# A two-layer encoder trunk: all full feed-forward groups by seven products, with the 256-column remainder moved forward

## The chip, the cores and the metric

The kernel runs on one core of a Trainium2 chip. The metric is the device time of one execution in microseconds; the time before is the median of three runs. The profile is that of one further execution.

## The reference

Two layers over `x` of shape (1, 256, 1024), float32. Each layer is a half feed-forward, a mixing block with two kinds of attention, and another half feed-forward; so there are four feed-forwards, and a final RMSNorm. What the change touches is the feed-forward with 2816 hidden columns, and the closing norm:

```python
def rms_norm(x, g):
    xf = x.astype(jnp.float32)
    y = xf * lax.rsqrt(jnp.mean(xf * xf, axis=-1, keepdims=True) + RMS_EPS)
    return (y * g.astype(jnp.float32)).astype(x.dtype)

def swiglu(h, w_gate, w_up, w_down):
    return (jax.nn.silu(h @ w_gate) * (h @ w_up)) @ w_down

for l in range(DEPTH):
    x = x + 0.5 * swiglu(rms_norm(x, ffn1_norm[l]), ffn1_w_gate[l], ffn1_w_up[l], ffn1_w_down[l])
    ...   # h @ w_in, windowed attention with sinks, differential attention, @ w_out
    x = x + 0.5 * swiglu(rms_norm(x, ffn2_norm[l]), ffn2_w_gate[l], ffn2_w_up[l], ffn2_w_down[l])
return rms_norm(x, final_norm)
```

## The kernel before

**Numbers in two parts.** Every weight and activation is split into a high and a low part (`fp32r`), and a product of two tiles is three matmuls: high by high, low by high, high by low. ScalarE makes the high part of a weight (a cast), VectorE the low part (a subtraction); `emit_split` (L175) does half a weight tile of 128 x 4 x 512 at a time, so a weight step is two casts and two subtractions of 128 x 1024.

**The list of weight steps.** `specs` holds all weight tiles in order of use. `weights()` (L233) hands out the next one and calls `ahead` (L212), which issues splits up to `look[0]` half-steps further (8 in the feed-forwards, `IN_FFN`, falling to 6, `IN_MIX`, also the value elsewhere), and loads up to ten steps ahead as long as fewer than six raw tiles (`N_RAW`) are alive. `Split.part` (L166) calls `ahead` again when the second half of a step is first used, unless the step is held. The split tiles lie in a pool of 28 (`N_S4`).

**The order on the engines.** `Kept` (L40) keeps the instructions of TensorE, ScalarE, VectorE and GpSimd in program order in the feed-forwards, so each engine works through its queue as the program lists it, and an instruction that waits holds back all behind it.

**A feed-forward** (`ffn`, L566) works on five groups of 512 hidden columns and a remainder of 256. Group 0 and group 1 are plain: 96 matmuls of 512 columns (two token halves, eight row blocks, gate and up, three each). Then `gate` takes the SiLU on ScalarE and `up` multiplies on VectorE; at the next group `turn` (L634) transposes the hidden block on TensorE and splits it, and `down` (L648) adds its products with the down weights to four PSUM banks, 24 matmuls for each half of the output columns.

**Seven products.** Groups 2 to 4 (`SEVEN`) go by `by_seven` (L598): gate and up, the two halves of the rows and the two token halves form a 2 x 2 block product done with seven block products in place of eight, 12 matmuls each. That needs four sums of activation blocks (`make_sums`, L333; each a VectorE operation, a ScalarE copy and a VectorE subtraction), four sums of weight blocks (two made by accumulating loads from GpSimd's queue, `gather`, two by VectorE in place, `plus`, L130), seven split weight tiles in place of four, and VectorE's additions of the products (`put`). In the last of these groups some of the splits are postponed (`late`).

**The end.** After group 4 stands the remainder of 256 columns (48 matmuls); then `ffn_end` (L704) and `ffn_close` (L725) do the down products of group 4 and of the remainder (`tail`, 12 matmuls for each half of the columns), with the residual sum and the first transposes of the next norm between. The last feed-forward has an ending of its own: `close` adds the residual and takes squares on ScalarE, `finish` multiplies with the final gain and stores. The first feed-forward also takes in `x` (`take_x`, L410) and, in group 1, the constants for the attention (`attention_constants`, L475).

Of the kernel before, what the change touches and what calls it, by code (L numbers as in the profile page):

```python
# [9 lines left out]
F32 = mybir.dt.float32  # L10
# [20 lines left out]
SEVEN = (2, 3, 4)  # L31
# [3 lines left out]
def trunk(ctx: ExitStack, tc: tile.TileContext, x, n1, g1, u1, d1, nm, w_in, sink,  # L35
# [254 lines left out]
    class Norm:  # L290


        def __init__(self, g0, sums=len(SEVEN) > 0):
# [39 lines left out]
        def make_sums(self):  # L333
# [76 lines left out]
    def take_x(k):  # L410
# [8 lines left out]
        elif k == 1:  # L419
            for e in (g, u, g, u):  # L420
                next(e)
            norm.pair(2)
            ahead(5)
            norm.pair(3)
        elif k == 2:
            ahead(7)
            for t in range(2):
                for h in range(2):
                    norm.squares(t, h * 512, 512)
            norm.stats()  # L430
            constants()
# [134 lines left out]
    def ffn(norm, aside=None, before=None, final=False):  # L566
# [31 lines left out]
        def by_seven(h, g):  # L598
# [10 lines left out]
            act.copy(m7, prod(norm.summed(2), weights(held=True)))  # L609
            hT = turn(h, 2)  # L610
# [6 lines left out]
            p5 = prod(norm.summed(0), weights())  # L617
            late = g == max(SEVEN)
            p6 = prod(norm.summed(1), weights(look[0] - 5 if late else 0, late))
# [12 lines left out]
            return h  # L632
# [15 lines left out]
        def down(hT, g, h, w):  # L648
            tokens(accs[h], [None] * (2 * g) + hT, w, 4 * g, last=(FC - 1, G4 - 1) if final and h else FC - 1)

# [17 lines left out]
        for n in range(1, NGRP):  # L668
            sums = norm.make_sums() if n + 1 == min(SEVEN, default=0) else iter(())
            if n in SEVEN:  # L670
                look[0] = IN_FFN - max(0, n - 2)
                h = by_seven(h, n)
                continue
            gs = [bank(), bank()]
            tokens(gs, norm.xs, weights(), 0)
            hT = turn(h, 2)
            norm.copies()
            tokens(gs, norm.xs, weights(), 4)
            g = gate(gs)
            next(sums, None)  # L680
            us = [bank(), bank()]
            for k0 in (0, 4):
                tokens(us, norm.xs, weights(), k0)
                next(sums, None)
            h = hidden(g, us)
            for hh in range(2):
                down(hT, n - 1, hh, weights())
                if hh == 0:
                    next(sums, None)
                    if aside is not None:  # L690
                        aside()
                        aside = None
# [8 lines left out]
    BY_TOKENS = [(k, t) for t in range(2) for k in range(2)]  # L701
    G4 = 4 * (NGRP - 1)

    def ffn_end(parts, last):  # L704

        accs, hT, rest = parts
        hT = [None] * (2 * (NGRP - 1)) + hT
        hE = []
        look[0] = IN_MIX
        w = {0: weights()}  # L710

        def group(h, order, a=None, c=slice(None), first=0):
            tokens(a or accs[h], hT, w[h], G4, first=first, last=last[h], order=order, cols=c)

        def tail(h, order=BY_TOKENS, a=None, c=slice(None)):
            tokens(a or accs[h], [None] * (2 * NGRP) + hE, w["rest"], 4 * NGRP, last=last[h], order=order, cols=c, h=h)

        group(0, [(k, t) for k in range(3) for t in range(2)])
        hE.extend(rest())
        group(0, [(3, t) for t in range(2)])  # L720
        w["rest"] = weights()
        w[1] = weights(2)
        return group, tail

    def ffn_close(parts, nxt):  # L725
        group, tail = ffn_end(parts, (FC - 1, G4 + 3))
        res = Residual(nxt, parts[0])
        group(1, [(0, t) for t in range(2)])
# [9 lines left out]
        group(1, [(2, t) for t in range(2)])  # L738
        group(1, [(3, t) for t in range(2)])
# [231 lines left out]
    fss = const.tile([P, 2, 4], F32, name="fss")  # L971
    gf = []

    def final_gain():
        gf.append(blk(F32))
        sp.dma_start(gf[0].rearrange("p a n -> p (a n)"), nf.partition_broadcast(P))
        pool.memset(fss, 0.0)


    for l in range(DEPTH):  # L980
        final = l == DEPTH - 1
        parts = ffn(norm, attention_constants, take_x) if l == 0 else ffn(norm)
        norm_m = Norm(16 + l * 8, False)
        ffn_close(parts, norm_m)
        norm2 = Norm(32 + l * 8)
        mix(l, norm_m, norm2)
        parts = ffn(norm2, final_gain if final else None, final=final)
# [3 lines left out]


    def close(t, c0, n, acc):
# [4 lines left out]
        act.activation(jk[:, :n], xv, AF.Square, accum_out=fss[:, t, c0 // 256:c0 // 256 + 1])  # L998
# [3 lines left out]
    def finish(t):  # L1002
        rf = tmp("rf", 2, (P, 1))
        dve.tensor_reduce(rf, fss[:, t], axis=mybir.AxisListType.X, op=ALU.add)
        dve.tensor_scalar(rf, rf, 1.0 / D, EPS, op0=ALU.mult, op1=ALU.add)
        pool.tensor_tensor(rf, rf, mhalf[:, 0:1], op=ALU.pow)
# [3 lines left out]
        for j in range(2):  # L1010
            sp.dma_start(out[0, t * P:(t + 1) * P, j * 512:(j + 1) * 512], ob[:, j])
# [5 lines left out]
    tail(0)  # L1017
    for t in range(2):
        close(t, 0, 512, accs[0][t])
    group(1, [(k, 0) for k in (2, 3)])  # L1020
    tail(1, [(k, 0) for k in range(2)])
    close(0, 512, 512, accs[1][0])
    finish(0)
    for c in (0, 256):
        acc = bank()[:, 0:256]
        cols = slice(c, c + 256)
        group(1, [(k, 1) for k in range(4)], [None, acc], cols, G4)
        tail(1, [(k, 1) for k in range(2)], [None, acc], cols)
# [32 lines left out]
```

## Time and profile before

| | |
|---|---|
| median of three runs | 940.94 us (940.77 to 941.16) |
| the profiled execution | 938.1 us, span 936.3 us |
| TensorE busy | 922.1 us, 4796 matmuls, granted clock 0.997 |
| VectorE busy | 757.3 us |
| ScalarE busy | 573.2 us |
| HBM read | 192.71 MB |

The span is from the first to the last instruction; the execution's own time is 1.8 us longer. Busy times of engines overlap. In answers by stretch, each row gives a stretch of the span, then for each engine its busy time and number of instructions, then TensorE's granted clock, the DMA share and GB/s. In answers in order of time, a row gives start, length, engine, line, operation, output and inputs, number of instructions, and in brackets the engine's idle time before it and what ended it. All engine instructions bear the line of the helper `Kept` (L50), so they are told apart by their tiles: `w` split weights, `raw` weights as loaded, `s` activations and hidden blocks, `q` and `v` sums of activations, `tmp` intermediate results, `ps` PSUM banks, `xk` the residual stream.

### The profile page before, as it was taken

The page shows a single profiled execution, that of the slowest core. Times are in us where ns is not written, and L with a number is a line of the kernel's source. Part 1 is how long each engine was busy: PE and PEld are TensorE (multiplying, and loading weights), DVE is VectorE, ACT ScalarE, POOL GpSimd, SP SyncE. Part 2 cuts the span into 40 slices and gives each one's busy share as a digit, 9 for nine tenths or more (in the row PEclk, how much of TensorE's full clock was granted, in tenths as well). Part 3 has the DMA queues.
Part 4 walks back from the last instruction along what each step waited for, and adds up shares of the span by engine and source line. Part 5 has one row for each costly group of instructions (what it writes and reads, how often), then busy time and mean ns, then how long its engine had stood idle before and what let it go on. Part 6 is the DMA issues. An engine that isn't in the chain of part 4 may idle for free.

```text
span 936.3 us, 12676 instructions
## 1 busy us (share of the span) xinstructions
PE 922.1 (98%) x4796; PEld 782.2 (84%) x4796; DVE 757.3 (81%) x1066; ACT 573.2 (61%) x901; POOL 51.3 (5%) x73
## 2 busy tenths in 40 slices
PE   8999999999999999999999999999999999999997
PEld 6788778899898888888888888888999888888886
DVE  6679999859866588999866799996697566799992
ACT  6847675548745666576475565665577476466562
POOL 0400100000000000100001000000000001001001
PEclk9999999999999999999999999999999999999999
DMA  9986897928425857797667597887462467697821
GB/s 336 355 219 159 247 289 249 270 91 225 136 91 180 249 156 225 206 288 256 240 227 221 135 288 202 240 284 217 150 193 91 135 205 202 166 299 204 249 91 46
DMA packets 110893, 194.58 MB, mean 208 GB/s; under 512 B 3566, under 2 KB 31280, under 8 KB 110832
## 3 DMA queue, kind: packets, MB, share of 16 engines
q1 hardware_dynamic: 96816, 167.27, 53.3%
q0 software_dynamic: 12928, 25.46, 15.4%
q10 hardware_dynamic: 1088, 1.05, 0.3%
q8 instruction: 37, 0.61, 0.3%
q14 instruction: 24, 0.20, 0.1%
HBM read 192.71 MB, written 1.05 MB: 207 GB/s over the span
## 4 chain that ended last, share of the span: by engine, by line
PE 92%; DMA 4%; DVE 1%; ACT 1%; issue 1%; SPq 0%; ACTq 0%; POOLq 0%; POOL 0%; DVEq 0%
PE ps L50 92%; DMA raw<-in_ffn_w_up_dram 2%; DMA raw<-in_ffn_w_gate_dram 2%; DVE w L50 1%; DMA xk<-in_x_dram 1%; ACT w L50 0%; DVE tmp L50 0%; ACT junk L50 0%; DVE s L50 0%; ACT tmp L50 0%; SPq L152 0%; ACT L50 0%; ACTq L50 0%; DVE xk L50 0%; POOLq L1056 0%
## 5 line engine op out<-in xcount | busy, mean ns | idle before, releaser
L50 PE MATMUL ps<-w,s 128*128 128x512 f32 (+1 forms) x2754 | 642.1, 391 | 2.1 <-ACT tmp L50 2.1
L50 PEld LDWEIGHTS ps<-w,s 128*128 128x128 f32 x2754 | 512.7, 189 | 107.8 <-ACT tmp L50 2.6
L50 DVE TENSOR_TENSOR w<-raw,w 128x1024 fp32r<-128x1024 f32 (+1 forms) x440 | 460.8, 1093 | 57.0 <-ACT w L50 55.8
L50 ACT CAST w<-raw 128x1024 fp32r<-128x1024 f32 (+1 forms) x440 | 391.1, 948 | 85.8 <-DVE raw L50 71.0
L50 PE MATMUL ps<-w,q 128*128 128x512 f32 x432 | 101.9, 389 | 0.0
L50 PEld LDWEIGHTS ps<-w,q 128*128 128x128 f32 x432 | 81.1, 188 | 16.8
L50 PE MATMUL ps<-s,w 128*128 128x256 f32 x672 | 84.1, 285 | 0.0
L50 PEld LDWEIGHTS ps<-s,w 128*128 128x128 f32 x672 | 81.7, 192 | 1.1
L50 ACT ACTIVATE s<-ps,gcol 128x256 fp32r<-128x256 f32 (+1 forms) x80 | 31.5, 488 | 48.0 <-PE ps L50 48.0
L50 ACT CAST s<-ps 128x512 fp32r<-128x512 f32 x48 | 26.1, 593 | 51.9 <-PE ps L50 51.9
L50 DVE TENSOR_TENSOR raw<-raw,raw 128x1024 f32<-128x1024 f32 x48 | 56.4, 1216 | 0.0
L50 DVE TENSOR_TENSOR s<-ps,s 128x512 fp32r<-128x512 f32 x48 | 31.0, 684 | 27.1 <-ACT s L50 27.1
L50 POOL DMA_DIRECT2D raw<-in_ffn_w_up_dram x24 | 31.0, 1293 | 354.9 <-DVE w L50 163.2
L50 PE MATMUL ps<-ident,s 128*128 128x128 f32 x304 | 40.2, 274 | 1.4 <-DVE s L50 1.3
L50 PEld LDWEIGHTS ps<-ident,s 128*128 128x128 f32 x304 | 35.0, 141 | 7.2 <-DVE s L50 2.8
L50 ACT ACTIVATE tmp<-tmp,r 128x512 f32<-128x512 f32 x24 | 17.3, 722 | 35.5 <-DVE tmp L50 35.5
L50 ACT ACTIVATE s<-s,negm 128x256 f32<-128x256 f32 x64 | 31.9, 500 | 5.4 <-DVE negm L50 5.2
L50 PE MATMUL ps<-w,v 128*128 128x512 f32 x144 | 34.6, 389 | 0.0
L50 ACT CAST q<-tmp 128x512 fp32r<-128x512 f32 x20 | 12.4, 620 | 35.0 <-DVE tmp L50 34.9
L50 PEld LDWEIGHTS ps<-w,v 128*128 128x128 f32 x144 | 27.0, 188 | 5.6
L50 DVE SCALAR_TENSOR_TENSOR s<-ps,gcol,s 128x256 fp32r<-128x256 f32 x48 | 20.3, 478 | 12.3 <-ACT s L50 12.3
L50 DVE TENSOR_TENSOR xk<-xk,ps 128x512 f32<-128x512 f32 (+1 forms) x25 | 14.2, 598 | 17.6 <-PE ps L50 17.6
(107 smaller groups left out, 426.1 us busy)
## 6 DMA issues: line engine op xcount, KB each, us to landing
raw<-in_ffn_w_down_dram SPq DMA_DIRECT2D x44, 1024.0 KB, 6.0
raw<-in_ffn_w_gate_dram SPq DMA_DIRECT2D x39, 1024.0 KB, 5.9
raw<-in_ffn_w_up_dram SPq DMA_DIRECT2D x39, 1024.0 KB, 5.6
raw<-in_ffn_w_up_dram POOLq DMA_DIRECT2D x24, 1024.0 KB, 11.2
raw<-in_w_in_dram SPq DMA_DIRECT2D x14, 1024.0 KB, 5.5
raw<-in_ffn_w_gate_dram SPq DMA_DIRECT2D x8, 512.0 KB, 6.4
raw<-in_ffn_w_up_dram SPq DMA_DIRECT2D x8, 512.0 KB, 7.4
raw<-in_w_in_dram SPq DMA_DIRECT2D x8, 512.0 KB, 6.8
```

Of the source, the lines that this page charges most:

```text
L50: ins = issue(*a, **k)
```

## The change

All four groups 1 to 4 go by seven products in every feed-forward. The order becomes: group 0, the remainder of 256 columns, groups 1 to 4; its hidden block is kept (`hE`) and its down products come at the end, ahead of and between those of group 4. The four sums of activations are made during the remainder's stage, two in its middle and two behind it, in another order. In the first feed-forward three of the four squares are taken earlier, the look-ahead is 6 from group 2 on, and the attention's constants are made in `ffn_close`. In the last one the squares are summed on VectorE in one instruction that also multiplies, the factor of the mean is put into the gain by GpSimd, and the stores go out on two queues.

```diff
-            for g in range(1, NGRP):
-                downs = [down(g - 1, h) for h in range(2)]
-                if g in SEVEN:
-                    specs.extend(seven(wg[l], wu[l], g * 512, downs))
-                else:
-                    specs.extend(plain(w[l], g * 512, 512, k0, 4) for w in (wg, wu) for k0 in (0, 4))
-                    specs.extend(downs)
             for k0 in (0, 4):
...
                 specs.append(Step(4, 512, gu_moves))
-            specs.append(down(NGRP - 1, 0))
+            for g in range(1, NGRP):
+                specs.extend(seven(wg[l], wu[l], g * 512, [down(g - 1, h) for h in range(2)]))
             specs.append(plain(wd[l], 0, D, 4 * NGRP, 2))
-            specs.append(down(NGRP - 1, 1))
+            specs.extend(down(NGRP - 1, h) for h in range(2))
...
+            make(t1, t0, ALU.subtract)
+            yield
             s1 = make(b1, t1, ALU.subtract)
             yield
             s2 = make(s1, t0, ALU.add)
             yield
-            make(t1, t0, ALU.subtract)
-            yield
             make(b0, s2, ALU.subtract)
...
+            norm.squares(0, 0, 512)
             norm.pair(2)
+            norm.squares(1, 0, 512)
             ahead(5)
             norm.pair(3)
+            norm.squares(0, 512, 512)
         elif k == 2:
             ahead(7)
-            for t in range(2):
-                for h in range(2):
-                    norm.squares(t, h * 512, 512)
+            norm.squares(1, 512, 512)
...
-            hT = turn(h, 2)
+            hs = turn(h, 1 if g == 1 else 2)
+            if g > 1:
+                hT = hs
...
+        norm.copies()
+
+        sums = norm.make_sums()
         gu = [bank(), bank()]
         tokens(gu, norm.xs, weights(), 0)
         hT = turn(h, 2)
+        for _ in range(2):
+            next(sums)
         tokens(gu, norm.xs, weights(), 4)
         h = hidden(gate([b[:, 0:256] for b in gu]), [b[:, 256:512] for b in gu])
-        return accs, hT, lambda: turn(h, 1)
+        for _ in sums:
+            pass
+        hE, h = by_seven(hT, h, 1)
+        for n in range(2, NGRP):
+            look[0] = IN_FFN - (n - 2) if before is not take_x else IN_MIX
+            h = by_seven(None, h, n)[1]
+        look[0] = IN_MIX
+        return accs, hE, lambda: turn(h, 2)
...
+    def ffn_close(parts, nxt, aside=None):
+        accs, hE, turn_ = parts
+        res = Residual(nxt, accs)
+        we = weights(1)
+        tail(accs[0], hE, we, 0)
+        hT = turn_()
+        if aside is not None:
+            aside()
+        group(accs[0], hT, weights(1), ALL)
         for t in range(2):
             res.add(0, t)
-        tail(1)
-        ahead(2 * at["use"] - 2 + look[0])
-        group(1, [(1, t) for t in range(2)])
+        tail(accs[1], hE, we, 1)
+        w = weights()
+        group(accs[1], hT, w, ALL[:2])
         for j in range(2):
             nxt.pair(j)
         res.squares(0)
-        group(1, [(2, t) for t in range(2)])
-        group(1, [(3, t) for t in range(2)])
+        group(accs[1], hT, w, ALL[2:])
...
-        act.activation(jk[:, :n], xv, AF.Square, accum_out=fss[:, t, c0 // 256:c0 // 256 + 1])
+        s_ = tmp("tot", 4, (P, 1))
+        dve.tensor_tensor_reduce(out=jk[:, :n], in0=xv, in1=xv, scale=1.0, scalar=tot[t], op0=ALU.mult, op1=ALU.add,
+                                 accum_out=s_)
...
-        dve.tensor_reduce(rf, fss[:, t], axis=mybir.AxisListType.X, op=ALU.add)
-        dve.tensor_scalar(rf, rf, 1.0 / D, EPS, op0=ALU.mult, op1=ALU.add)
-        pool.tensor_tensor(rf, rf, mhalf[:, 0:1], op=ALU.pow)
+        pool.tensor_tensor(rf, tot[t], mhalf[:, 0:1], op=ALU.pow)
...
-        for j in range(2):
-            sp.dma_start(out[0, t * P:(t + 1) * P, j * 512:(j + 1) * 512], ob[:, j])
-
-    accs = parts[0]
-    group, tail = ffn_end(parts, ((FC - 1), FC - 1))
+        for j, q in enumerate((act, sp)):
+            q.dma_start(out[0, t * P:(t + 1) * P, j * 512:(j + 1) * 512], ob[:, j])
+
+    accs, hE, turn_ = parts
+    we = weights(1)
+    tail(accs[0], hE, we, 0)
+    tail(accs[1], hE, we, 1, (-1, FC - 1))
     dve.tensor_tensor(xk[:, 1, 512:D], xk[:, 1, 512:D], accs[1][1], op=ALU.add)
-    group(1, [(k, 0) for k in range(2)])
-    tail(0)
+    hT = turn_()
+    group(accs[0], hT, weights(), ALL)
...
```

More of the change, by code (lines that the diff above doesn't have):

```diff
@@ L564, in late, with ffn @@
                 self.nxt.stats()
-    def ffn(norm, aside=None, before=None, final=False):
+    def ffn(norm, before=None):
         def silu(out_, acc, t):
@@ L648, in down @@
         def down(hT, g, h, w):
-            tokens(accs[h], [None] * (2 * g) + hT, w, 4 * g, last=(FC - 1, G4 - 1) if final and h else FC - 1)
+            tokens(accs[h], [None] * (2 * g) + hT, w, 4 * g, last=-1)
         gs, us = [bank(), bank()], [bank(), bank()]
@@ L667, in ffn @@
         h = hidden(g, us)
[L668 to L692, printed above, removed]
+        norm.copies()
+        sums = norm.make_sums()
         gu = [bank(), bank()]
@@ L701, in trunk @@
+        return accs, hE, lambda: turn(h, 2)
     BY_TOKENS = [(k, t) for t in range(2) for k in range(2)]
+    ALL = [(k, t) for k in range(4) for t in range(2)]
     G4 = 4 * (NGRP - 1)
[L704 to L728, printed above, removed]
-        tail(0)
+    def tail(accs, hE, w, h, last=-1):
+        tokens(accs, [None] * (2 * NGRP) + hE, w, 4 * NGRP, last=last, order=BY_TOKENS, h=h)
+    def group(accs, hT, w, order, c=slice(None), first=0):
+        tokens(accs, [None] * (2 * (NGRP - 1)) + hT, w, G4, first=first, last=G4 + 3, order=order, cols=c)
+    def ffn_close(parts, nxt, aside=None):
[7 more added lines that the diff above has]
+        group(accs[0], hT, weights(1), ALL)
@@ L990, in trunk @@
             ffn_close(parts, norm)
+    tot = [tmp("tot", 4, (P, 1)) for _ in range(2)]
+    for t in range(2):
+        dve.memset(tot[t], D * EPS)
     def close(t, c0, n, acc):
@@ L1025, in trunk @@
         acc = bank()[:, 0:256]
[L1026 to L1028 removed]
+        group([None, acc], hT, w, [(k, 1) for k in range(4)], slice(c, c + 256), G4)
         close(1, 512 + c, 256, acc)
```

32 lines of the change are left out of this document (16 added, 16 removed).

## The prediction

> **What bounds the kernel now.** I read the page first, then the chain, then the busy time by stage, then the order in time around the places where one engine waits for another.
>
> ```profile
> span 936.3 us, 12676 instructions
> ...
> PE 922.1 (98%) x4796; PEld 782.2 (84%) x4796; DVE 757.3 (81%) x1066; ACT 573.2 (61%) x901; POOL 51.3 (5%) x73
> ...
> PE 92%; DMA 4%; DVE 1%; ACT 1%; issue 1%; SPq 0%; ACTq 0%; POOLq 0%; POOL 0%; DVEq 0%
> ```
>
> TensorE carries 92% of the chain, so a matmul removed should be time removed. VectorE's 81% looks like room. It is a mean over unlike stages, so the next view is busy time by stage: two seven-product groups of the first feed-forward, then of the second feed-forward group 0 and the seven-product groups 2, 3 and 4.
>
> ```profile
> core 0: us, PE busy (x) PEld busy (x) DVE busy (x) ACT busy (x) POOL busy (x), PEclk, DMA share, GB/s
> ...
> 99.60:131.90 32.30, 31.32 (x142) 25.58 (x141) 31.73 (x34) 20.02 (x23) 2.55 (x2) 1.00 0.87 245
> 131.90:163.40 31.50, 31.04 (x141) 25.35 (x140) 31.40 (x35) 19.16 (x23) 0.00 (x0) 1.00 0.84 255
> ```
>
> ```profile
> 293.60:315.50 21.90, 21.90 (x104) 18.20 (x103) 15.04 (x22) 16.96 (x28) 0.70 (x1) 1.00 0.72 232
> ...
> 350.60:381.40 30.80, 30.80 (x141) 25.60 (x140) 26.61 (x27) 17.99 (x21) 2.57 (x2) 1.00 0.84 232
> 381.40:412.30 30.90, 30.90 (x142) 25.64 (x141) 30.39 (x32) 19.46 (x23) 2.57 (x2) 1.00 0.82 241
> 412.30:443.10 30.80, 30.80 (x142) 25.59 (x141) 30.66 (x34) 20.26 (x24) 0.00 (x0) 1.00 0.82 247
> ```
>
> In the second feed-forward TensorE never stops, but VectorE is busy 26.61 of 30.80 us in group 2 and then 30.39 of 30.90 and 30.66 of 30.80. From the second seven-product group on VectorE is full. The change puts a fourth such group in that row. So the question is how much VectorE is behind, and the rows for that are the end of `up` (VectorE's last two products of a group, `s<-tmp,hr,tmp`) against the transposes (`ident`) of the next group that read them.
>
> ```profile
> 383.88 1.41 DVE L50 SCALAR_TENSOR_TENSOR s<-tmp,hr,tmp 128x512 f32<-128x512 f32 x2
> ...
> 415.53 1.42 DVE L50 SCALAR_TENSOR_TENSOR s<-tmp,hr,tmp 128x512 f32<-128x512 f32 x2
> ```
>
> ```profile
> 356.86 2.98 PE L50 MATMUL ps<-w,s 128*128 128x512 f32 x12
> ...
> 373.27 11.04 PE L50 MATMUL ps<-w,s 128*128 128x512 f32 x48
> 384.15 2.89 PE L50 MATMUL ps<-w,q 128*128 128x512 f32 x12
> 386.88 1.03 PE L50 MATMUL ps<-ident,s 128*128 128x128 f32 x8
> ...
> 417.71 1.03 PE L50 MATMUL ps<-ident,s 128*128 128x128 f32 x8
> ```
>
> Group 2's `up` ends at 385.29 and is read at 386.88: 1.59 us to spare. Group 3's ends at 416.95 and is read at 417.71: 0.76 us. TensorE's period is 417.71 - 386.88 = 30.83 us, VectorE's 416.95 - 385.29 = 31.66 us, and in that group the look-ahead had just been cut from 8 to 7, which saved VectorE one split. These are the last margins of the old kernel.
>
> **Part by part: TensorE.** Group 1 becomes seven products: 84 matmuls in place of 96. The pitch is (384.15 - 373.27) / 48 = 0.227 us, so 12 x 0.227 = 2.72 us for each of four feed-forwards, 10.9 us in all. The order of the stages and the places of the down products move matmuls without adding any.
>
> **VectorE.** What a group holds there:
>
> ```profile
> L50 DVE TENSOR_TENSOR w<-raw,w 128x1024 fp32r<-128x1024 f32 x18 | 21.3, 1217 | 0.4 <-ACT w L50 0.3
> L50 DVE TENSOR_TENSOR raw<-raw,raw 128x1024 f32<-128x1024 f32 x4 | 4.7, 1216 | 0.0
> L50 DVE TENSOR_TENSOR tmp<-ps,tmp 128x512 f32<-128x512 f32 x3 | 2.0, 682 | 0.0
> L50 DVE TENSOR_TENSOR tmp<-tmp,ps 128x512 f32<-128x512 f32 x3 | 2.0, 680 | 0.0
> ```
>
> A converted group splits 7 weight tiles, not 4 (6 more half-tile splits x 1.217 = 7.3 us), makes two sums of weights in place (4 x 1.216 = 4.9) and combines the products (7 x 0.68 = 4.8): 17.0 us more per feed-forward, against 2.72 us less of TensorE. None of it hides by itself where VectorE is full; it hides only if VectorE is ahead when the row of four begins. The next rows price a split in a full queue and the end of group 4.
>
> ```profile
> 443.20 1.41 DVE L50 SCALAR_TENSOR_TENSOR s<-tmp,hr,tmp 128x512 f32<-128x512 f32 x2
> 444.53 6.90 DVE L50 TENSOR_TENSOR w<-raw,w 128x1024 fp32r<-128x1024 f32 x6
> ...
> 448.52 1.03 PE L50 MATMUL ps<-ident,s 128*128 128x128 f32 x8
> ...
> 451.35 1.28 DVE L50 TENSOR_TENSOR s<-ps,s 128x512 fp32r<-128x512 f32 x2
> ```
>
> A split takes 6.90 / 6 = 1.15 us. VectorE's periods are therefore: with the look-ahead constant, 31.66 + 1.15 = 32.8 us; with one step less, 31.66; and for the last group, with its postponed splits, 444.61 - 416.95 = 27.66.
>
> **Entry into group 1.** Up to 325.06 us (the first group's `turn`) the old trace holds for the new order too, since TensorE has the same 24 matmuls ahead of it.
>
> ```profile
> 322.52 1.04 PE L50 MATMUL ps<-ident,s 128*128 128x128 f32 x8
> ```
>
> ```profile
> 323.77 1.29 DVE L50 TENSOR_TENSOR s<-ps,s 128x512 fp32r<-128x512 f32 x2 [3.10 <-ACT s L50]
> ...
> 330.40 0.69 DVE L50 TENSOR_TENSOR tmp<-s,s 128x512 f32<-128x512 f32 x1
> 331.77 0.69 DVE L50 TENSOR_TENSOR q<-tmp,q 128x512 fp32r<-128x512 f32 x1 [0.69 <-ACT q L50]
> ```
>
> ```profile
> 357.37 1.29 DVE L50 TENSOR_TENSOR s<-ps,s 128x512 fp32r<-128x512 f32 x2 [0.99 <-ACT s L50]
> ```
>
> One sum of tokens costs VectorE 332.46 - 330.40 = 2.06 us, 0.69 of it waiting for ScalarE's copy. Before, the four lay between splits over 35 us of group 1. After, they stand in pairs inside 11 us of the 256-column stage: two sums (4.1), two splits (2.3), two short `up` (about 1, half the shape of the long ones' 0.7 each), two sums (4.1), three splits (3.4), the `turn` of the narrow hidden block (0.7), and about 0.4 of waiting for casts: 325.0 + 16 = 341.0. TensorE ends that stage at 322.5 + 0.8 + 24 x 0.227 = 328.8, and starts the third product after two products and four transposes at 334.6. So VectorE is 341.0 - 334.6 = 6.4 us behind where in group 2 of the old kernel it was 358.66 - 356.86 = 1.8. It is 4.6 us later, and the spare was 1.6: the first transposes wait 3.0 us.
>
> **The row of four**, feed-forwards 2 and 3. Group 1 to 2: 3.0 us (above). Group 2 to 3, look-ahead 8 both times: 32.8 - 30.8 = 2.0. Group 3 to 4, cut to 7: 31.66 - 30.83 = 0.8. After group 4 the transposes come 12 matmuls later than the downs' end, not 24 as before, so TensorE arrives after 30.83 - 2.72 = 28.1 us and `up` after 27.66: no wait, 0.45 to spare. But the transposed block is now used at once, by `group(accs[0], ...)`; before, 24 matmuls stood between. Four splits stand ahead of it in VectorE's queue: 4 x 1.15 + 0.6 = 5.2 us after `up`, of which the 0.45 and the transposes' 0.9 are covered: 3.8 us. Sum 9.6 - 2.72 = +6.9 us each, +13.8 for both.
>
> **Feed-forward 4.** Both tails stand ahead of the transposes, so the last wait is 3.8 - 2.72 = 1.1: 3.0 + 2.0 + 0.8 + 1.1 - 2.72 = +4.2. The closing is shorter:
>
> ```profile
> 928.87 4.54 SPq L1011 DMA_DIRECT2D out_dram<-s  x4
> ...
> 929.79 0.42 DVE L50 TENSOR_TENSOR xk<-ps,xk 128x256 f32<-128x256 f32 x1 [0.58 <-PE ps L50]
> ...
> 931.27 0.56 POOL L50 TENSOR_TENSOR rf<-rf,mhalf 128x1 f32<-128x1 f32 x1 [3.18 <-DVE rf L50]
> ```
>
> Between the last add (ends 930.21) and the power (931.27) lie 1.06 us of ScalarE's square, its read-out and two small VectorE steps; one multiply-and-sum on VectorE, about as long as that add, with its read-out leaves some 0.6. With the last store on a queue of its own (one issue less, about 0.4) I take -0.9. Sum +3.3.
>
> **Feed-forward 1.** It has waits of its own now: the excess of the two stages over 30.83, 1.5 + 0.7 = 2.2, and this at the end of group 0:
>
> ```profile
> 31.00:33.20 2.20, 0.16 (x1) 0.16 (x2) 1.85 (x2) 2.18 (x3) 2.20 (x6) 1.00 1.05 387
> 33.20:36.70 3.50, 3.50 (x9) 2.72 (x10) 2.17 (x2) 3.50 (x5) 3.05 (x16) 0.51 1.06 376
> ```
>
> TensorE does 0.16 us of work in 2.20 (the gate's SiLU stands behind four squares), and then the granted clock is 0.51 for 3.5 us. With three squares moved ahead the wait goes (2.1 us) and, I take it, the slow clock with it (1.7). The new waits: 3.0; group 2 has two splits less (look-ahead 6), 30.5, so none and 0.3 gained; group 3 32.8, 1.7; group 4 27.66 + 1.15 - 28.1 = 0.7; the block at the end 5.2 - 0.9 = 4.3. Sum 9.7 - 2.72 - 2.1 - 1.7 - 2.2 = +1.0. The attention constants move behind the last transposes; they hide beside 48 matmuls, and cost up to 3 us if they do not.
>
> **Queues.** Eight more accumulating loads of 1 MB go through POOL. The DMA share in seven-product stages is 0.82 to 0.87 where the start shows 1.05, so I take zero; a late one costs at most what feed-forward 1 shows, 1 to 2 us. The final gain now waits on POOL before the last feed-forward, with its loads already issued: zero, or 1 us. A third product in group 1 may wait for the bank that ScalarE's copy frees: 0 to 1 us each, mostly inside the 3.0.
>
> **The sum**: +1.0 + 6.9 + 6.9 + 3.3 = +18.1 us. The profiled execution took 938.1 us, 1.8 outside its span, and would take 956.2. The median shown, 940.94, is 2.8 above that; 940.9 + 18.1 gives 959 us.
>
> **Rivals.** *Caught up at the entry*: if the sums hide and group 1 starts as group 2 did, each feed-forward loses 3.0 and the 1.6 of spare comes off the next wait: 4.6 x 4 = 18.4, and the time is 941, no change. For it speaks only that the old sums were hidden; against it that they wait on ScalarE in pairs now. *All hidden, faster*: the look-ahead of four to five weight steps swallows the fourth group. It decides where VectorE's surplus over four groups stays under its margin at the entry; then the waits stay out: -10.9 - 2.1 - 1.7 - 0.9 = -15.6, 925 us. For it: TensorE stood still nowhere in feed-forward 2. Against: 1.59 and then 0.76 us to spare after only two groups, and the uncovered block at the end, which no look-ahead helps. *Clock drops*: waits of 3.8 us may bring the half clock of the rows above behind each of the first three feed-forwards, 1.7 us each: 964 us. The Trainium skill ("TensorE: Matmul & The Clock Gate", Part 1) has the clock halved after an idle window of about 3.4 us; here an idle of 2.1 us was enough, so the measured row decides, and by either the wait is long enough.
>
> **How the numbers follow.** VectorE-bound as summed 0.68, clock drops on top 0.13, caught up 0.06, all hidden 0.13. The likeliest gives 959. Upward, bank waits (up to 4), constants (3) and the clock (5) are not all paid at once: 969. Downward, I take three quarters of the entry's 18.4 as hidden: 945; that leaves no change and 925 outside, less than 2 in 10 together. A difference under 0.2% (1.9 us) is no change. Faster 0.14, same 0.05, slower 0.81.
>
> **What would show it.** TensorE idle before the transposes of groups 2 and 3 with VectorE as releaser, and before the first matmuls of the last group's downs; VectorE above 30.3 of every 30.8 us in all four groups; the second and third feed-forwards some 7 us longer than before; no 2.1 us gap at 31 us. It is wrong if TensorE's idle stays near 14 us in all, or if VectorE has idle time at the start of group 1.

## The result and the profile after

The changed kernel takes 989.78 us (median of 4 executions, 988.47 to 990.68) against 940.86 us of the kernel before on the same chip: ratio 1.0519, 95% interval 1.05 to 1.0537. It is slower, as forecast, but by 49 us where 18 were forecast, and outside the range of 945 to 969. The profiled execution has a span of 988.9 us, 52.6 more than the one before.

The page of the changed kernel, with the rows that answer to those of before (the last is the chain by engine and line):

```profile
span 988.9 us, 12741 instructions
...
PE 934.1 (94%) x4742; PEld 781.1 (79%) x4742; DVE 822.9 (83%) x1142; ACT 594.7 (60%) x921; POOL 63.5 (6%) x81
...
PE 48%; DVE 21%; DMA 18%; issue 10%; ACT 3%; POOLq 0%; ACTq 0%; DVEq 0%; POOL 0%
PE ps L49 48%; DMA raw<-in_ffn_w_up_dram 18%; DVE w L49 12%; DVE tmp L49 5%; ACT w L49 2%; DVE s L49 2%; DVE raw L49 2%; DMA xk<-in_x_dram 0%; ACT s L49 0%; ACT q L49 0%; DVE q L49 0%; DVE xk L49 0%; ACTq L49 0%; DVEq L49 0%; ACT junk L49 0%
```

The records hold 54 matmuls fewer (48 of them the fourth group's four times 12), yet TensorE is busy for longer; one reason is that some of them ran at half clock. Its share of the chain falls from 92% to 48%. VectorE has 21%, which fits the forecast's mechanism, but the loads of the up weights have 18%, which the forecast had costed at nothing. The list of waits says the same; each row gives the total, the number of waits and the longest. First before, then after:

```profile
ACT w L50 <- DMA raw<-in_ffn_w_up_dram: 10.0, 9, 2.8
...
PE ps L50 <- DVE s L50: 1.3, 3, 0.7
```

```profile
ACT w L49 <- DMA raw<-in_ffn_w_up_dram: 49.0, 22, 10.1
...
PE ps L49 <- DVE s L49: 27.2, 24, 7.5
PE ps L49 <- DVE tmp L49: 11.2, 10, 2.4
```

To see where the time lies I cut each profiled execution at the first transposes of the residual (`ident,xk`) ahead of feed-forwards 2, 3 and 4. Before, these start at 299.85, 478.04 and 757.54 us. The mixing blocks in the first and third stretch hardly change, so the differences are those of the feed-forwards (the fourth with the closing):

| difference to before, us | FF1 | FF2 | FF3 | FF4 and closing | sum |
|---|---|---|---|---|---|
| forecast | +1.0 | +6.9 | +6.9 | +3.3 | +18.1 |
| after | +19.9 | +13.7 | +10.8 | +8.2 | +52.6 |
| a1, accumulating loads left out | +3.2 | +7.5 | +8.6 | +5.4 | +24.7 |
| d3, a seventh raw tile, nothing left out | +15.8 | +7.6 | +8.6 | +5.1 | +37.1 |
| a3, VectorE's weight sums left out | +7.8 | -1.2 | -1.4 | -0.5 | +4.7 |
| c3, new order, group 1 plain | +1.8 | +3.8 | +5.7 | +2.8 | +14.1 |
| f1, all remedies | +7.7 | +2.8 | +2.6 | +5.1 | +18.2 |
| f2, new order, group 1 plain, end mended | -2.8 | +0.4 | +0.3 | +2.1 | +0.1 |

(The profiled execution of before was 2.8 us under its median; on that account every measured sum is 2.8 us too high.) More than a third of the loss is in FF1, which was forecast to lose 1.0.

**Inside feed-forward 2.** Stretches between the transposes of groups 1 to 4, columns as in the forecast's tables:

```profile
354.10:388.60 34.50, 32.46 (x138) 26.08 (x135) 31.43 (x34) 23.11 (x27) 2.57 (x2) 0.95 0.81 224
388.60:422.10 33.50, 31.84 (x141) 25.41 (x140) 32.16 (x35) 20.98 (x25) 2.57 (x2) 1.00 0.87 248
422.10:455.30 33.20, 31.53 (x140) 25.48 (x140) 31.19 (x34) 19.94 (x24) 2.60 (x2) 1.00 0.89 250
```

TensorE's own period is 30.8. So the stages are 3.7, 2.7 and 2.4 us longer than that (the first with half clock in it: a mean of 0.95), where 3.0, 2.0 and 0.8 were forecast, and VectorE is *not* busy all the time: it is idle for 3.1, 1.3 and 2.0 us of them. Something makes VectorE wait. In order of time, one such round: GpSimd, ScalarE, VectorE and TensorE, each with its idle time before the instruction and what ended it:

```profile
398.26 1.29 POOL L49 DMA_DIRECT2D raw<-in_ffn_w_up_dram  x1 [20.34 <-DMA raw<-in_ffn_w_up_dram]
...
410.64 4.84 ACT L49 CAST w<-raw 128x1024 fp32r<-128x1024 f32 x5 [1.98 <-DMA raw<-in_ffn_w_up_dram]
...
411.73 2.36 DVE L49 TENSOR_TENSOR w<-raw,w 128x1024 fp32r<-128x1024 f32 x2 [1.20 <-ACT w L49]
...
422.18 0.33 PE L49 MATMUL ps<-ident,s 128*128 128x128 f32 x1 [0.74 <-DVE s L49]
```

and the chain of the same round (start, length, what):

```profile
391.49 1.23 DVE w L49
392.73 4.97 DMA raw<-in_ffn_w_up_dram
...
398.26 12.31 DMA raw<-in_ffn_w_up_dram
...
410.64 1.06 ACT w L49
```

This is a loop. VectorE's split at 391.49 gives a raw tile back; only then a plain load can go out (4.97 us), only on its landing the accumulating load (12.31 us), only on that ScalarE's cast, and on the cast VectorE's next splits. So VectorE, late by its volume, is made later by a load that its own lateness put off. The same pieces stand on the chain in the groups before and after (358.90 with 5.03 and 364.50 with 12.59 us; 426.22 with 5.01 and 432.11 with 12.77). The chain of the kernel before has one such round, in feed-forward 1 (109.92 with 5.01, 115.55 with 11.55).

The end block came as forecast: four splits stand ahead of the `turn`, and TensorE waits 0.29 and 2.91, 3.2 us in all (3.8 forecast).

```profile
483.53 4.62 DVE L49 TENSOR_TENSOR w<-raw,w 128x1024 fp32r<-128x1024 f32 x4
...
488.07 1.28 DVE L49 TENSOR_TENSOR s<-ps,s 128x512 fp32r<-128x512 f32 x2
...
488.81 0.79 PE L49 MATMUL ps<-w,s 128*128 128x512 f32 x1 [2.91 <-DVE s L49]
```

**The start of feed-forward 1** in the changed kernel:

```profile
30.85 1.46 POOL L49 DMA_DIRECT2D raw<-in_ffn_w_up_dram  x1 [29.35 <-DMA raw<-in_ffn_w_up_dram]
31.84 1.24 POOL L49 TENSOR_TENSOR r<-ms,mhalf 128x2 f32<-128x2 f32 x1
...
33.85 7.33 PE L49 MATMUL ps<-w,s 128*128 128x512 f32 x24 [2.79 <-ACT tmp L49]
44.45 1.99 ACT L49 CAST w<-raw 128x1024 fp32r<-128x1024 f32 x2 [10.07 <-DMA raw<-in_ffn_w_up_dram]
...
48.70 2.32 PE L49 MATMUL ps<-ident,s 128*128 128x128 f32 x8 [7.52 <-DVE s L49]
```

The forecast had the wait at 31 us going with the moved squares. It is still there, 2.79 us, with another cause: group 1's first accumulating load now stands on GpSimd's queue *ahead of the power* that the norm needs, and GpSimd stands idle in front of it for 29.35 us, until a plain load has landed; the power's input was ready at 27.13. Then ScalarE waits 10.07 us for that accumulating load, the first splits behind it, `up` behind them, and TensorE 7.52 us for `up`. In the kernel before, the first accumulating load goes out 12 us later and behind the power, and none of this was in the way:

```profile
29.65 0.72 POOL L50 TENSOR_TENSOR r<-ms,mhalf 128x2 f32<-128x2 f32 x1 [28.14 <-DVE ms L50]
...
43.21 1.38 POOL L50 DMA_DIRECT2D raw<-in_ffn_w_up_dram  x1 [0.95 <-ACT s L50]
```

### The profile page after: what moved, and what is told of

Read it like the earlier page. It is cut to its first block, busy times and chain, and to the rows that moved or that the text cites. A ratio compares the mean times of both kernels' runs of the same rounds, so it can differ in the third digit from the quotient of the medians.

```text
span 988.9 us, 12741 instructions
## 1 busy us (share of the span) xinstructions
PE 934.1 (94%) x4742; PEld 781.1 (79%) x4742; DVE 822.9 (83%) x1142; ACT 594.7 (60%) x921; POOL 63.5 (6%) x81
## 3 DMA queue, kind: packets, MB, share of 16 engines
HBM read 201.10 MB, written 1.05 MB: 204 GB/s over the span
## 4 chain that ended last, share of the span: by engine, by line
PE 48%; DVE 21%; DMA 18%; issue 10%; ACT 3%; POOLq 0%; ACTq 0%; DVEq 0%; POOL 0%
PE ps L49 48%; DMA raw<-in_ffn_w_up_dram 18%; DVE w L49 12%; DVE tmp L49 5%; ACT w L49 2%; DVE s L49 2%; DVE raw L49 2%; DMA xk<-in_x_dram 0%; ACT s L49 0%; ACT q L49 0%; DVE q L49 0%; DVE xk L49 0%; ACTq L49 0%; DVEq L49 0%; ACT junk L49 0%
## 5 line engine op out<-in xcount | busy, mean ns | idle before, releaser
L49 PE MATMUL ps<-w,s 128*128 128x512 f32 x2508 | 604.0, 398 | 22.7 <-DVE s L49 10.8
L49 PEld LDWEIGHTS ps<-w,s 128*128 128x128 f32 x2508 | 475.7, 192 | 126.9 <-DVE s L49 12.2
L49 DVE TENSOR_TENSOR w<-raw,w 128x1024 fp32r<-128x1024 f32 (+1 forms) x464 | 488.6, 1100 | 53.3 <-ACT w L49 52.0
L49 ACT CAST w<-raw 128x1024 fp32r<-128x1024 f32 (+1 forms) x464 | 416.3, 953 | 148.7 <-DVE raw L49 89.0
L49 PE MATMUL ps<-w,q 128*128 128x512 f32 x576 | 136.4, 390 | 3.6 <-DVE tmp L49 3.6
L49 PEld LDWEIGHTS ps<-w,q 128*128 128x128 f32 x576 | 107.8, 188 | 28.2 <-issue 5.9
L49 POOL DMA_DIRECT2D raw<-in_ffn_w_up_dram x32 | 41.6, 1298 | 526.0 <-DMA raw<-in_ffn_w_up_dram 187.1
L49 DVE TENSOR_TENSOR raw<-raw,raw 128x1024 f32<-128x1024 f32 x64 | 75.3, 1219 | 0.0
L49 ACT ACTIVATE s<-ps,gcol 128x256 fp32r<-128x256 f32 (+1 forms) x80 | 31.4, 483 | 57.5 <-PE ps L49 54.6
L49 PE MATMUL ps<-w,v 128*128 128x512 f32 x192 | 46.1, 389 | 0.0
L49 DVE TENSOR_TENSOR tmp<-ps,tmp 128x512 f32<-128x512 f32 x48 | 32.8, 684 | 0.0
## 6 DMA issues: line engine op xcount, KB each, us to landing
raw<-in_ffn_w_up_dram POOLq DMA_DIRECT2D x32, 1024.0 KB, 12.6
```

What stands on the lines that cost most here:

```text
L49: ins = issue(*a, **k)
```

## Experiments

### The loads, or VectorE's volume?

**a1**: every accumulating load left out (`gather` does nothing). **a2**: only the 16 of them that hang on the second weight (`behind=None`).

```diff
-                pool.dma_start(raws[to], w[k], accum_op=ALU.add)
+                pass
```

> The changed kernel without its 32 accumulating loads from GpSimd's queue (both kinds; the sums of weights B+C and A+B are left out). Theory L (late loads): in every seven-product group the cast of the second weight tile waits for a chain of slot freed, load, accumulating load (about 5 + 12.6 us), and all of ScalarE and VectorE waits behind it; without the accumulating loads the kernel falls to at most 962 us, the 7.5 us wait at 41 us and the 3 us wait at 31 us go, and no cast waits over 2 us for a load. Theory V (VectorE's volume, the prediction's): only the two early waits and their slow clock go (about 17 us, 972), the waits before the transposes of groups 2 to 4 stay as they are, 2 to 4 us each.

> The changed kernel without the accumulating load that stands ahead of the cast of the second tile (16 of 32; the sum B+C is left out), the other kind kept. Theory L: the same time as without both, within 3 us, since the other sum is wanted only five steps later. If the second kind holds the kernel too, or GpSimd's queue does, it stays 5 us or more above it. Theory V: about 972.

a1 took 962.32 us, ratio 1.0233 (1.0203 to 1.0262); a2 962.17, ratio 1.0231 (1.0201 to 1.0261). So these loads are worth 27.5 us, and leaving out half of them brings all of it. By the table, 16.7 us of it lie in feed-forward 1 and 11.2 in the other three.

```profile
ACT w L49 <- DMA raw<-in_ffn_w_up_dram: 0.9, 2, 0.6
...
PE ps L49 <- DVE s L49: 18.6, 23, 3.4
```

```profile
337.50:370.00 32.50, 31.17 (x137) 24.87 (x135) 31.34 (x34) 23.03 (x27) 0.00 (x0) 1.00 0.58 194
370.00:402.20 32.20, 31.26 (x140) 25.56 (x140) 32.06 (x35) 20.76 (x25) 0.00 (x0) 1.00 0.57 196
402.20:433.80 31.60, 31.20 (x140) 25.56 (x140) 31.12 (x34) 19.86 (x24) 0.00 (x0) 1.00 0.60 200
```

The first fence is a1's list of waits, the second its feed-forward 2, groups 1 to 3. With the loads out of the way the stages last 1.7, 1.4 and 0.8 us over TensorE's period, VectorE is nearly full (31.3, 32.1 and 31.1 us), and FF2 to FF4 lose 7.5, 8.6 and 5.4 where 6.9, 6.9 and 3.3 were forecast. The kernel that the forecast describes is this one, at 962. By itself a1 can't tell a wait from traffic, since the DMA share falls with the loads, to 0.57 to 0.60; d3 below can.

**a3**: VectorE's sums of weights in place left out, the loads kept.

```diff
-                    dve.tensor_tensor(t_, t_, x_, op=ALU.add)
+                    pass
```

> The changed kernel without VectorE's 64 in-place additions of weights (the sums are left out), 4.6 us less of VectorE in each of 16 groups. Theory V: VectorE's surplus over TensorE (2 us a group) is gone, the waits of the second, third and fourth feed-forward before the transposes go, 9 us each with the end: about 957 to 962 us. Theory L: the chain of loads still sets the cast of the second tile; the freed slots come 4.6 us earlier at the best, so part of the waits goes: 970 to 980.

942.84 us, ratio 1.0026 (1.0015 to 1.0038). The 64 sums are 75.3 us of VectorE's time; without them 47 us go, and feed-forwards 2 to 4 are *shorter* than before. What is left is the start (+7.8), which the volume does not explain:

```profile
ACT w L49 <- DMA raw<-in_ffn_w_up_dram: 16.9, 7, 10.0
...
PE ps L49 <- DVE s L49: 9.5, 5, 7.5
```

Either removal takes most of the loss, so they are not two separate sums but two links of the loop above.

**c2**: the same sums on GpSimd in place of VectorE (`pool.tensor_tensor`).

> The changed kernel with the 64 in-place sums of weights on GpSimd in place of VectorE. VectorE is relieved as in the run without them (942.8 us). If GpSimd has the time (2.6 us each by the 1.29 us of its 128x512 sum, 10 us a group of 31) and its queue is no hindrance: 943 to 950. Rival: GpSimd works its queue in order, so a sum that waits for the second accumulating load holds up the next group's first one, and its cast waits longer than now: 985 or more.

1121.84 us, ratio 1.1918 (1.1873 to 1.1963). GpSimd needs 2.28 times as long for one (2777 against 1219 ns), and ScalarE's casts wait 173.6 us for these sums in all; GpSimd's queue issues the accumulating loads as well:

```profile
L49 POOL TENSOR_TENSOR raw<-raw,raw 128x1024 f32<-128x1024 f32 x64 | 176.9, 2777 | 391.5 <-DVE w L49 391.5
```

**d3**: a seventh raw tile, so that a plain load need not wait for the split to give one back (the 28 split tiles become 26 to make room).

```diff
-N_RAW, N_S4 = 6, 28
+N_RAW, N_S4 = 7, 26
```

> The changed kernel with seven raw weight tiles in place of six, and 26 split tiles in place of 28 to make room. If the loads are late because a raw tile comes free late (theory L with V), one tile more starts them a step earlier, 3 to 5 us, and a third to a half of the waits of the second to fourth feed-forward behind accumulating loads goes, less what the two missing split tiles cost: 975 to 984. If only the transfer itself is slow, no change: 988 to 992.

974.81 us, ratio 1.0367 (1.0348 to 1.0387): 15.0 us back without taking anything out of VectorE's work. ScalarE's wait for the up weights falls from 49.0 to 11.1 us, of which 10.0 is the one at the start. This cuts the loop at its first link and shows that the raw tiles were the link: in FF2 to FF4 it loses 7.6, 8.6 and 5.1 us, as a1 does (7.5, 8.6, 5.4), with every load kept. In those three, what the accumulating loads cost was the missing tile.

```profile
ACT w L49 <- DMA raw<-in_ffn_w_up_dram: 11.1, 3, 10.0
```

### The start of feed-forward 1

**a4**: the first accumulating loads are held back until the power is on GpSimd's queue. **c1**: in FF1 the look-ahead is 4 until group 1, so that fewer splits stand ahead of `up`. **d4**: both.

```diff
+            norm.stats()
+            release()
...
-        look[0] = IN_FFN
+        look[0] = 4 if before is take_x else IN_FFN
```

> The changed kernel with the first accumulating load put into GpSimd's queue behind the power that makes the first norm's factor r, not ahead of it. If that load held r up, the 3.2 us wait at 31 us falls below 1 us and the half clock behind it goes (1.7 us). But the accumulating load then starts no earlier, and the cast that waits for it at 34 to 44 us ends no earlier either: the 7.5 us wait before the transposes grows by what is won. Both theories: 986 to 990.

> The changed kernel with the look-ahead of the first feed-forward at 4 during group 0 and the remainder (8 before), then 6. The cast that waits for the first accumulating load then stands behind the first group's products in both queues, not ahead of them. If the 7.5 us wait at 41 us comes from that order, it goes, and with it most of the 10.2 us of half clock behind it (5 us): 978 us. If the load is simply late whatever stands behind it, the wait only moves into group 1: 986 to 990. The wait of 3.2 us at 31 us stays in both.

> The changed kernel with both edits at the start: look-ahead 4 in the first feed-forward until group 1, and the first accumulating load behind the first norm's power. The 3.5 us wait at 31 us goes with its half clock on top of the 8.5 us of the first edit alone: 975 to 978. If the later accumulating load only moves the wait into group 1 again: 980 to 983.

a4: 990.36 us, ratio 1.0531 (1.0479 to 1.0582). The gap at 31 us is gone (0.30 us left) and the wait behind it grew to 11.49: the load came no earlier (30.95 us), so the rest only waited longer. c1: 981.3, ratio 1.0425 (1.0383 to 1.0467); the long wait becomes 3.33 us, the gap at 31 stays (3.14). d4: 977.92, ratio 1.04 (1.038 to 1.042); gap gone, 3.06 us left at 50 us, 11.9 us back in all. Holding the load back gives nothing by itself and 3.4 us once the splits are out of the way.

**c4**: the old order of the stages, with all four groups by seven products.

```diff
-SEVEN = (2, 3, 4)
+SEVEN = (1, 2, 3, 4)
```

> The old order of the stages and the old ending with all four groups by seven products, the four sums right behind group 0. Theory V with L: the fourth group does the harm, so the loss stays; the entry is worse by some 3 us, with the sums in one row and no remainder ahead, and the end is covered by 24 matmuls again (3.4 us won three times): 975 to 995. If the new order did the harm it is below 955.

986.43 us, ratio 1.0479 (1.0433 to 1.0525): nearly as slow as the new order, but not in the same places. Its start is worse (TensorE idle for 15.25 us until 46 us), and feed-forward 1 loses 24.7 us; feed-forwards 2 and 3 lose 7.1 and 7.8, where the changed kernel loses 13.7 and 10.8. So the fourth group costs time in either order; the new order is not free beside it, as the next runs show.

### The new order and its end block

**c3**: the new order, but group 1 plain. **d2**: c3 with the second tail (12 matmuls) put between the last transposes and the products that use them, and splits that stood ahead of the block in VectorE's queue postponed.

```diff
-            w = weights(look[0] - 3 if late else 0)
+            w = weights(look[0] - 3 if late else 0, late)
...
-        we = weights(1)
+        we = weights(3)
         tail(accs[0], hE, we, 0)
         hT = turn_()
...
+        we.held = True
+        tail(accs[1], hE, we, 1)
         group(accs[0], hT, weights(1), ALL)
...
-        tail(accs[1], hE, we, 1)
```

> The changed order of the stages, of the sums and of the ending with group 1 plain as before (groups 2 to 4 by seven products). Theory V with L (VectorE's surplus in the fourth such group frees slots late, and the accumulating load stretches it): the waits before the transposes of groups 2 and 3 are gone or below 1 us; what is left is the uncovered block at the end, up to 3.4 us three times, with its slow clock: 941 to 952. Rival (the order itself does the harm): above 965.

> The changed order with group 1 plain (954 us), and the last hidden block covered: the transposes ahead of the second tail, 12 matmuls between them and the block's first use, and the four splits that stood ahead of it in VectorE's queue postponed, two to behind it and two to its first use. If the uncovered block is what the order costs, its 3.4 to 3.9 us three times fall below 1 us each and the slow clock behind them goes: 940 to 944. If the block is late for another reason, it stays above 948.

c3: 954.3 us, ratio 1.0138 (1.0081 to 1.0194), and all TensorE's waits for hidden blocks are in the end blocks:

```profile
PE ps L49 <- DVE s L49: 10.6, 5, 3.4
```

Behind those of FF1 and FF3 the clock is halved for 3.4 us, so such a block costs 3.4 + 1.7; behind that of FF2 (2.90 us) it isn't. d2: 944.96, ratio 1.0047 (1.0029 to 1.0065); those waits are gone (the longest left is 0.9), 9.3 us back. Whether the tail or the postponed splits did it wasn't separated. In FF1 a new wait of 3.95 us stands in their place: the residual sums stand on VectorE behind the attention's constants and six splits.

### What the moved squares gained, and where it went

**d1**: the kernel before with the squares moved and the new closing. **f3**: the squares alone. **f4**: the closing alone.

> The kernel before with two parts of the change alone: three squares of the first norm taken earlier, and the closing (sum of squares on VectorE, factor in the gain, stores on two queues). No accumulating load stands ahead of the first norm's power here, so the 2.1 us wait at 31 us and the 1.7 us of half clock behind it should go, and 0.9 us at the close: 936 us. If the wait at 31 us has another cause than the squares it stays, and the time is 940.

> The kernel before with the three squares moved ahead and nothing else. Theory, the earlier start itself brings the 5.2 us stall at 71 us, since the loads that the first seven-product group needs do not come earlier: gap at 31 us gone, stall at 71 us there, 940.5 to 941.5 us. Rival, the stall came with the new closing (GpSimd's multiply of the final gain, one instruction more in its queue at the start): no stall at 71 us, 936 to 938 us.

> The kernel before with the new closing and nothing else. Theory: the start unchanged, no stall at 71 us, the end 0.9 us shorter, 939.5 to 940.5 us. Rival, the stall at 71 us belongs to the closing: 943 to 946 us.

d1: 940.21 us, ratio 0.9996 (0.9987 to 1.0005). f3: 941.01, 1.001 (1.0001 to 1.0019). f4: 940.94, 1.0003 (0.9994 to 1.0012). In d1 the gap at 31 us is gone, but not the time: the transposes of the first group come 3.6 us earlier (36.57 against 40.21), and at 71 us it is all given back:

```profile
70.50 1.03 PE L50 MATMUL ps<-ident,s 128*128 128x128 f32 x8
76.47 3.78 PE L50 MATMUL ps<-w,s 128*128 128x512 f32 x8 [4.93 <-ACT tmp L50]
```

f4 has a stall of 3.90 us there too, with its squares where they were (its first group's transposes came at 37.33), so neither of the two theories for that stall holds as written. What the four kernels share is ScalarE's cast behind the first accumulating load. In the kernel before, f4, f3 and d1 it stands at:

```profile
56.79 2.00 ACT L50 CAST w<-raw 128x1024 fp32r<-128x1024 f32 x2 [2.75 <-DMA raw<-in_ffn_w_up_dram]
```

```profile
57.98 2.00 ACT L50 CAST w<-raw 128x1024 fp32r<-128x1024 f32 x2 [6.82 <-DMA raw<-in_ffn_w_up_dram]
```

```profile
59.28 2.00 ACT L50 CAST w<-raw 128x1024 fp32r<-128x1024 f32 x2 [8.04 <-DMA raw<-in_ffn_w_up_dram]
```

```profile
58.25 2.00 ACT L50 CAST w<-raw 128x1024 fp32r<-128x1024 f32 x2 [7.87 <-DMA raw<-in_ffn_w_up_dram]
```

TensorE's next products start 18.2 us behind that cast in all four (75.02, 76.19, 77.50 and 76.47 us), however early TensorE arrives. The load goes out at 43.2 to 45.2 us, and the DMA share in all four is 1.05 or more from 20 to 60 us. That the loads are what holds this point is read from the traces; a kernel with less to load in the first 60 us wasn't tried. Why f4's start was earlier than that of before is open: its edit touches nothing there, and each trace is one execution.

### Both causes at once, and the order without the fourth group

**f1**: the changed kernel with d3's seventh raw tile, d4's start, d2's covered end and the attention's constants behind the residual sums. **f2**: d2 with the seventh raw tile and the constants moved in the same way.

> The changed kernel with all three remedies at once: the first accumulating load behind the statistics with the shorter look-ahead at the start (alone -11.9 us), a seventh raw tile (alone -15.0), the end block covered by both tails with the attention's constants behind the residual sums (alone, with a plain group 1, -9.3). Theory, VectorE's volume plus the wait for accumulating loads are the whole loss: the remedies overlap little, so 989.8 - 11.9 - 15.0 - 9.3 = 953.6 us, within 948 to 958, with the stalls that are left named VectorE and no long wait of ScalarE on the weight loads. Rival, the remedies move one and the same wait: the best of them alone counts, 968 to 975 us. Rival, nothing but the waits stood between the change and its gain: 926 to 932 us.

> The new order with a plain group 1 and the covered end (945.0 us), with the attention's constants put behind the residual sums and a seventh raw tile. Theory: the 4.3 us stall in the first feed-forward's end and half of its slow clock (1.7) go, nothing else; 938 to 940 us, faster than the kernel before by 0.1 to 0.3%. Rival, VectorE's work is only put elsewhere, as the gap at 31 us was: 944 to 946 us.

f1: 956.33 us, ratio 1.0173 (1.0158 to 1.0189). Of the 49 us, 33.5 are back; the three remedies alone gave 36.2 (9.3 of it with a plain group 1), so they hardly overlap. The granted clock is back at 0.997. The stages of FF2 (transposes at 341.98, 374.51, 406.71, 438.32) last 32.5, 32.2 and 31.6 us: the same as in a1, with nothing left out this time. VectorE is busy for 31.4, 32.1 and 31.1 us of them: this is the floor that its volume sets. What feed-forward 1 still loses (7.7 us) has other waits in it, one of 3.1 us for a cast at 53 us, and wasn't followed further. The waits for hidden blocks that are left are many and small:

```profile
PE ps L49 <- DVE s L49: 9.9, 22, 0.9
```

f2: 938.49 us (11 executions), ratio 0.9983 (0.9974 to 0.9992) against 940.45 of before. It is the one version here that beats both kernels, by 0.2% and with an interval that leaves out 1: with the end covered and the fourth group plain the new order costs nothing more. Whether the order or the seventh raw tile brings the gain isn't shown, since the old order with seven raw tiles wasn't run; nor is which of f2's two additions to d2 ended the stall in FF1.

## Why the forecast was wrong

**The entry and the row of four: right in kind and nearly in size.** A group too many for VectorE, TensorE waiting for `up` group after group, two to three microseconds at a time. VectorE's lateness at the entry came as summed: in a1 its `turn` of the narrow block ends at 344.09, 6.2 us behind the start of TensorE's product at 337.91 (6.4 forecast). With the loads out of the way (a1, and f1 with them in) the excesses are 1.7, 1.4 and 0.8 for 3.0, 2.0 and 0.8 forecast, so the first was too large. The sum for a1 is 24.7 against 18.1: half clock for 17 us behind three of its end blocks, which the forecast kept out of its sum as a rival, is in it, so that the total comes so near is in part luck.

**The end block: right**, 3.2 us for 3.8 in feed-forward 2. c3 and d2 show that covering it brings 9.3 us, half clock included and the new stall of 3.95 in FF1 already paid.

**The step that failed is "Queues"**: "so I take zero; a late one costs at most what feed-forward 1 shows, 1 to 2 us". It measured 27.5 us (a1): 11.2 in feed-forwards 2 to 4, and 16.7 in feed-forward 1, which is the next point. The argument looked at the DMA share, which in feed-forward 2 is indeed no different (0.81 to 0.89 against 0.82 to 0.87). But there the loads are not short of bandwidth: f1's stages are as short as a1's at shares of 0.74 to 0.91. They are short of a free tile and then take their latency: 5.0 us for the plain load and 12.3 for the accumulating one, one after the other, counted from the moment that VectorE returns a tile. The row for it was in the profile of before, and it wasn't read:

```profile
raw<-in_ffn_w_up_dram POOLq DMA_DIRECT2D x24, 1024.0 KB, 11.2
```

The 1 to 2 us were read off feed-forward 1, whose stage from 99.6 to 131.9 us holds the one such round of the kernel before; in the changed kernel every feed-forward has one or more on the chain. A stall that goes back into the queue which frees buffers had to be followed for one more turn.

**Feed-forward 1: wrong, +1.0 against +19.9.** "With three squares moved ahead the wait goes": it went where the first seven-product group stays late (c3, d1) or its accumulating load is held behind the power (a4, d4); in the change itself it stayed. The forecast moved the group's splits and matmuls in time but not its accumulating load, which now stands on GpSimd's queue ahead of the power, and whose landing at 44 us holds ScalarE. Here the DMA share is 1.06 to 1.10 from 20 to 44 us, so that this load is slow for want of bandwidth isn't excluded. a1 recovers 16.7 of the 19.9.

**Clock drops**, a rival at 964 us, had the right mechanism and too small a count: 1.7 us for each of three waits. The changed kernel spends at half clock:

```profile
44.40:54.60 10.20, 5.78 (x17) 4.71 (x18) 7.84 (x9) 7.84 (x15) 5.59 (x22) 0.50 0.70 172
...
194.60:201.40 6.80, 5.07 (x12) 4.01 (x13) 5.99 (x15) 1.81 (x3) 0.00 (x0) 0.50 1.09 306
382.30:385.70 3.40, 3.40 (x9) 2.64 (x9) 3.40 (x4) 0.86 (x2) 0.00 (x0) 0.50 1.09 257
488.10:494.90 6.80, 6.09 (x14) 4.79 (x15) 5.79 (x7) 2.46 (x3) 0.00 (x0) 0.50 1.07 361
```

and 3.4 us each at 34, 573 and 679. TensorE's busy time in these seven stretches is 30.5 us; at half clock half of it is lost, by estimate some 15 us.

**The closing**: -0.9 forecast. From the last add to the power it takes 0.61 us in d1 against 1.06, as forecast (0.6). The other part, 0.4 from the second store queue, didn't come: from the power to the end it is 5.31 us against 5.03. The whole edit can't be told from no change (f4).

**The attention's constants** "hide beside 48 matmuls": in the changed kernel they do; with the end block covered (d2) they and the splits behind them hold the residual sums, and TensorE stands still for 3.95 us, more than the 3 us that the forecast gave them.

## What to carry to other kernels

Where an engine that is full also gives back the buffers that loads wait for, a step that it does later is paid twice: once for the work, and once for the latency of the load that starts later; read the time from issue to landing, not the DMA share. When a stage is moved forward, move every instruction that it issues in each queue, and look at what now stands behind each of them, above all behind a DMA issue that waits. An edit that fills the last slack should be tried together with a buffer more, since that separates the two costs (here 15 us for one tile).

## What the runs showed of the hardware

An accumulating load of 1 MB took 12.6 us from issue to landing (median of 32), a plain load of the same size and weight 5.4 (median of 39):

```profile
raw<-in_ffn_w_up_dram SPq DMA_DIRECT2D x39, 1024.0 KB, 5.4
raw<-in_ffn_w_up_dram POOLq DMA_DIRECT2D x32, 1024.0 KB, 12.6
```

With seven raw tiles the median of the accumulating load was 9.5 us (d3, f1) and that of the plain one 6.3 and 6.7, so neither is a constant; what sets them wasn't separated. Half clock came in stretches of 3.4, 6.8 and 10.2 us, the multiples of one window. In the changed kernel the seven stretches start at 34.2, 44.4, 194.6, 382.3, 488.1, 573.5 and 679.3 us: the last lies 645.1 us behind the first, 189 times 3.413, and the five between lie 3, 47, 102, 133 and 158 times that behind it, to 0.1 us. Idle times of 2.79 us (at 34) and 2.04 (at 381) were enough to bring it on:

```profile
381.35 4.58 PE L49 MATMUL ps<-w,s 128*128 128x512 f32 x12 [2.04 <-DVE tmp L49]
```

These twelve take 4.58 us, where 2.9 is usual. The Trainium skill ("TensorE: Matmul & The Clock Gate", Part 1) gives a free-running window of 3413 ns, and the lengths agree; it also has a whole idle window ahead of the drop, where the traces show shorter idle times. That the window runs by itself fits the common grid of the seven starts, and c3, where an idle of 2.90 us at 461 us brought no half clock at all: continued from its drop at 179.0 us, the grid of that run has a boundary at 462.3, inside this idle time. How much idle time within one window is enough isn't settled here.
